# Six down-projection matmuls ahead of a slab's last two products, and another token order for the first two row blocks

## The chip, the core and the metric

The kernel runs on one core of a Trainium2 chip. A core has a matrix engine (TensorE, called PE in the profile, with its weight loads as PEld), a vector engine (DVE), a scalar engine (ACT), a GpSimd engine (POOL) and a sync engine (SP) that here issues all large DMAs. The engines run side by side and wait for each other through semaphores. SBUF is the on-chip memory; PSUM holds the sums of the matmuls in eight banks. The metric is the device time of one execution in microseconds (us); lower is better.

## What is computed

Two layers, each a gated feed-forward block, a mixer (convolution, linear recurrence, windowed attention) and a second gated feed-forward block, each followed by a residual layer norm, on 512 tokens of width 1024 in float32. The change touches the feed-forward blocks alone, of which there are four:

```python
def _swiglu(x, wg, wu, wd):
    return (jax.nn.silu(x @ wg) * (x @ wu)) @ wd
...
    for l in range(DEPTH):
        h = 0.5 * _swiglu(x, ffn_w_gate[l, 0], ffn_w_up[l, 0], ffn_w_down[l, 0])
        x = _layernorm(ALPHA * x + h, ln_g[l, 0], ln_b[l, 0])
...
        h = 0.5 * _swiglu(x, ffn_w_gate[l, 1], ffn_w_up[l, 1], ffn_w_down[l, 1])
        x = _layernorm(ALPHA * x + h, ln_g[l, 2], ln_b[l, 2])
```

`x` is 512 x 1024, `wg` and `wu` are 1024 x 2816, `wd` is 2816 x 1024.

## The kernel before

**Numbers in two parts.** A float32 product is made from three matmuls: each operand is split into a rounded part (`wh`, `hH`: the high part) and the rest (`wl`, `hL`). `split` (L128) does this with an ACT cast (L130) and then a DVE subtraction (L131), so a weight tile costs one load by DMA, one ACT cast and one DVE subtraction before PE can use both parts.

**Slabs.** A feed-forward block works through its 2816 hidden columns in three slabs (`SLABS`, L43) of 4, 4 and 3 pairs of 256 columns (the very first pair of a block is done apart). Four blocks of three slabs make twelve slab ends; in eight of them another slab of the same block follows, and four are the last of their block (`fin`, L486).

**First half of a slab: products.** Each pair's gate and up projections are made by a scheme that needs seven products of half-size blocks in place of eight. The products have names: p1, p2, q6, p5, p7, p4, q3. Each is 24 matmuls (L481 to L483) with 256 moving columns. They share PSUM banks: p1, q6, p7 and p4 of one pair add up one after the other in one bank, p5 and q3 in another, and p2 has a third (L503). Between two products of a bank its sum so far is taken out: by an ACT copy after p1 (L510), q6 (L515), p7 (L517) and p4 (L520), and by DVE after p7 (L518, from the bank of p5) and q3 (L523). `seq` (L550 to L554) is the order of the products. Inside a slab the p4 and q3 of one pair come after the p1 of the next pair. For the last pair of a slab there is no next pair, and the order ends p5, p7, p4, q3, so that p4 follows p7 directly in the same bank.

**Weights of the products** are made ready (`prep`, L427) `AHEAD` = 3 products early (L557 to L560): when p5 of the last pair runs, q3's weights are prepared, and nothing is left to prepare in `seq`. The raw gate and up weights of a pair lie in buffers of `tpool` (L408, DMAs of L411, two per buffer); as soon as one of them comes free, the next slab's raw weights are fetched into it.

**Second half of a slab: the down projection.** For each row block f of `wd` (128 of its rows, 4 KB each; a slab has 8, 8 or 6) the block is loaded and split (`load_rows`, L386, its DMA is L365), and for each t of the four blocks of 128 tokens `rowmm` (L453) adds six matmuls with 512 moving columns into the two PSUM banks `ys[t]`: two of `hL` with `wh`, then four of `hH` with `wl` and `wh`. In the trace these are L107. The eight banks of `ys` are all the banks there are. The first row block of a slab is f0, its hidden columns are those of the slab's first pair, finished long before the slab's end. In the last slab the last four row blocks go by tokens instead of by f, into the layer norm.

**Order and buffers.** The program is written as one sequence; when it is built, a list scheduler puts the instructions of each engine in an order by priority (place in the program) and by when it believes that they can start. Each engine then runs its own list strictly from the front, and SP its DMAs. Buffers of a pool (`wpool` has 15 of 4 KB per partition: raw, high and low weights, the products' outputs `o` and sums) are handed out in the program's order of first use: a tile gets its buffer only after every tile that is first written earlier in the program has got one. The raw, `wh` and `wl` of a row block are three such tiles; `ob`, the tile which the ACT copy after p7 (L517) writes first, is another.

Of the kernel before, what the change touches and what calls it, by code (L numbers as in the profile page):

```python
# [18 lines left out]
P = 128  # L19
D = 1024  # L20
S = 512
NT = S // P
# [30 lines left out]
def tile_hymba(  # L53
# [39 lines left out]
    def nm(s):  # L93
        uid[0] += 1
        return f"{s}_{uid[0]}"

    def bank():
        return psum.tile([P, 512], F32, tag="ps", name=nm("ps"))
# [7 lines left out]
    def mm(o, a, b, start, stop):  # L106
        nc.tensor.matmul(o, a, b, start=start, stop=stop)  # L107
# [25 lines left out]
    def transposed(dst, q, j, src):  # L133

        pt = bank()
        for c in range(4):
            nc.tensor.transpose(pt[:, c * P:(c + 1) * P], src[:, c * P:(c + 1) * P], ident)  # L137
        sl = slice(j * P, j * P + P)
        split(dst[q][:, 0, :, sl], dst[q][:, 1, :, sl], pt.rearrange("p (c t) -> p c t", c=4))
# [179 lines left out]
    class Start:  # L319
# [6 lines left out]
        def load(self, n=1, pool=None):  # L326
            for _ in range(n):
                self.pairs.append(self.thunks.pop(0)(pool))
# [57 lines left out]
    def load_rows(src, c, pool=None):  # L386
        return load(src[c * P:(c + 1) * P, :], pool)
# [65 lines left out]
    def rowmm(ys, a, w, first, last):  # L453
        ah, al = a
        wh, wl = w
        for hf in range(2):
            sl = slice(hf * 512, (hf + 1) * 512)
            mm(ys[hf], al, wh[:, sl], first, False)
        for hf in range(2):
            sl = slice(hf * 512, (hf + 1) * 512)  # L460
            mm(ys[hf], ah, wl[:, sl], False, False)
            mm(ys[hf], ah, wh[:, sl], False, last)

    def ffn(l, i, idx, start, nxt, last, hooks={}):
        wd = w_down[l, i]
# [8 lines left out]
        def product(step, n, pb, first):  # L474
            src, q = A[step]
            wh, wl = pairs[n].ready.pop(step)
            for g in range(2):
                o = pb[:, g * HALF:(g + 1) * HALF]
                for k in range(4):
                    st = first and g == 0 and k == 0  # L480
                    nc.tensor.matmul(o, wl[:, g, k, :], src[q][:, 0, k, :], start=st, stop=False, skip_group_check=True)  # L481
                    nc.tensor.matmul(o, wh[:, g, k, :], src[q][:, 1, k, :], start=False, stop=False, skip_group_check=True)  # L482
                    nc.tensor.matmul(o, wh[:, g, k, :], src[q][:, 0, k, :], start=False, stop=k == 3, skip_group_check=True)  # L483

        for si, (n0, n1) in enumerate(SLABS):
            fin = si == len(SLABS) - 1  # L486
            f0, f1 = 2 * n0, 2 * n1
            hH = hpool.tile([P, HMAX, S], F32R, tag="hA", name=nm("hH"))
            hL = hpool.tile([P, HMAX, S], F32R, tag="hB", name=nm("hL"))

            def finish(n, which, tile_, s0):

                v = tile_.rearrange("p (b g s) -> p b g s", b=2, g=2)
                nc.scalar.activation(v[:, :, 0, :], v[:, :, 0, :], AF.Silu)
                nc.vector.tensor_tensor(v[:, :, 0, :], v[:, :, 0, :], v[:, :, 1, :], op=ALU.mult)
                f = 2 * (n - n0)
                sl = (slice(None), slice(f, f + 2), slice(s0, s0 + HALF))
                split(hH[sl], hL[sl], v[:, :, 0, :])

            def run(step, n):  # L500
                if step in ("p1", "p2", "p5"):
                    acc[step, n] = bank()
                pb = acc[{"p1": "p1", "q6": "p1", "p7": "p1", "p4": "p1", "p2": "p2", "p5": "p5", "q3": "p5"}[step], n]  # L503
                product(step, n, pb, step in ("p1", "p2", "p5"))
                if step == "p1":
                    outs[n] = [wpool.tile([P, D], F32, tag="w", name=nm("o")) for _ in range(2)]
                oa, ob = outs[n]
                lo, hi = slice(0, 512), slice(512, 1024)
                if step == "p1":
                    nc.scalar.copy(oa[:, lo], pb)  # L510
                elif step == "p2":
                    nc.vector.tensor_tensor(oa[:, lo], pb, oa[:, lo], op=ALU.add)
                    acc.pop(("p2", n))
                elif step == "q6":
                    nc.scalar.copy(oa[:, hi], pb)  # L515
                elif step == "p7":
                    nc.scalar.copy(ob[:, hi], pb)  # L517
                    nc.vector.tensor_tensor(ob[:, hi], acc["p5", n], ob[:, hi], op=ALU.subtract)  # L518
                elif step == "p4":
                    nc.scalar.copy(ob[:, lo], pb)  # L520
                    finish(n, 1, ob, HALF)
                elif step == "q3":
                    nc.vector.tensor_tensor(oa[:, hi], pb, oa[:, hi], op=ALU.subtract)  # L523
                    finish(n, 0, oa, 0)
                    acc.pop(("p5", n))
                    acc.pop(("p1", n))
                    outs.pop(n)

            m4 = []
            first = n0 + 1 if si == 0 else n0  # L530
            if si == 0:
# [18 lines left out]
            seq = []  # L550
# [4 lines left out]
            ready = 0  # L555
            for m, (step, n) in enumerate(seq):
                while ready < min(len(seq), m + 1 + AHEAD):  # L557
                    st, k = seq[ready]
                    pairs[k].prep(st)
                    ready += 1  # L560
                    if st == "p5" and k + 1 < n1:
                        pairs[k + 1].raw(0, 0)
                        pairs[k + 1].raw(1, 0)
                run(step, n)
                if m4:
                    transposed(sT, 2, 2 - len(m4), m4.pop(0))
                if step == "q3" and n in hooks:
                    hooks[n]()
            if fin:
                extra.pop()  # L570
            ys = [[bank(), bank()] for _ in range(NT)]

            def hpair(f, t):
                return hH[:, f - f0, t * P:(t + 1) * P], hL[:, f - f0, t * P:(t + 1) * P]

            flow = f1 - RESIDENT if fin else f1
            for f in range(f0, flow):
                w = load_rows(wd, f)
                for t in range(NT):
                    rowmm(ys[t], hpair(f, t), w, f == f0, f == f1 - 1)  # L580
            if not fin:
                for t in range(NT):
                    for hf, sl in enumerate(HS):
# [9 lines left out]
            def rows(t):  # L593
                for w, f in zip(ws, range(flow, f1)):
                    rowmm(ys[t], hpair(f, t), w, f == f0, f == f1 - 1)
                return ys[t]
# [332 lines left out]
    for l in range(DEPTH):  # L929
        phases += [(ffn, (l, 0, 3 * l), ffn_start(l, 0)), (mixer, (l, 3 * l + 1), mixer_start(l)),  # L930
                   (ffn, (l, 1, 3 * l + 2), ffn_start(l, 1))]
# [61 lines left out]
```

## Time and profile before

| | us |
|---|---|
| median of 3 runs | 1787.61 (1785.95 to 1791.46) |
| the profiled execution | 1785.95 |
| its span, first to last instruction | 1784.2 |
| mean granted TensorE clock | 0.994 of full speed |

A row of the profile names line, engine, operation, and out<-in tiles; L107 is the helper `mm`, so those rows are told apart by their tiles (`hH`, `hL` only occur in the down projection). A matmul row's duration overlaps the next one's: a stream's pace is the distance between two starts. A timeline row is: start, duration, engine, line, operation, tiles, shape, count, and in square brackets how long the engine had been idle and what ended that. A row with x4 merges four instructions. SP's rows are DMA issues; the transfer itself lasts longer.

### The profile page before, as it was taken

How to read it: one execution, taken by the hardware profiler on the slowest of the kernel's cores; microseconds unless marked ns; L12 is line 12 of the kernel's file. 1: busy time of each engine (PE TensorE's matmuls, PEld its weight loads, DVE VectorE, ACT ScalarE, POOL GpSimd, SP SyncE). 2: the span in 40 equal slices, each digit the busy share in tenths (PEclk: the TensorE clock that was granted, in tenths of full speed). 3: DMA queues.
4: the chain of work that ended last, by engine and by line, in shares of the span. 5: the costliest groups of instructions: out<-in, count | busy, mean ns of one | idle time of the engine just before them, and what ended most of it. 6: DMA issues, size and time to landing. Idle time of an engine off the chain costs nothing. (4 is left out here: it accounts for less than half of the span.)

```text
span 1784.2 us, 27912 instructions
## 1 busy us (share of the span) xinstructions
PE 1730.9 (97%) x11538; PEld 1564.1 (88%) x11538; DVE 1279.1 (72%) x1777; ACT 824.2 (46%) x1224; POOL 41.8 (2%) x76
## 2 busy tenths in 40 slices
PE   8999999999999999999999999999999999999997
PEld 8988989988579989989889899898876899899896
DVE  5856756769977856857588567575898877587475
ACT  4543443533854643534445345254458445255252
POOL 0200000010000000000000000000000000000000
PEclk9999999999999999999999999999999999999999
DMA  5341542322322442422334324223321244135122
GB/s 157 108 142 57 159 135 69 108 79 66 98 82 63 130 141 60 128 97 72 107 92 122 130 71 136 78 72 108 106 66 60 71 130 149 57 104 165 44 87 72
DMA packets 236840, 177.34 MB, mean 99 GB/s; under 512 B 9524, under 2 KB 219561, under 8 KB 236713
## 3 DMA queue, kind: packets, MB, share of 16 engines
q1 hardware_dynamic: 236712, 175.55, 32.3%
q8 instruction: 91, 1.49, 0.3%
q14 instruction: 37, 0.30, 0.1%
HBM read 171.33 MB, written 3.67 MB: 98 GB/s over the span
## 5 line engine op out<-in xcount | busy, mean ns | idle before, releaser
L131 DVE TENSOR_TENSOR wl<-raw,wh 128x1024 fp32r<-128x1024 f32 x268 | 324.8, 1221 | 151.8 <-ACT wh L130 118.0
L481 PE MATMUL ps<-xT,wl 128*128 128x256 f32 x1280 | 359.1, 281 | 9.4 <-ACT o L517 8.8
L482 PE MATMUL ps<-xT,wh 128*128 128x256 f32 x1280 | 356.9, 279 | 0.0
L483 PE MATMUL ps<-xT,wh 128*128 128x256 f32 x1280 | 356.7, 279 | 0.0
L130 ACT CAST wh<-raw 128x1024 fp32r<-128x1024 f32 x268 | 278.5, 1049 | 122.3 <-DMA raw<-in_ffn_w_down_dram 58.6
L131 DVE TENSOR_TENSOR wl<-t,wh 128x1024 fp32r<-128x1024 f32 x160 | 195.8, 1226 | 144.1 <-ACT wh L130 118.4
L107 PE MATMUL ps<-wl,hH 128*128 128x512 f32 x704 | 274.7, 390 | 1.1 <-DVE wl L131 1.1
L107 PE MATMUL ps<-wh,hH 128*128 128x512 f32 x704 | 274.3, 390 | 0.0
L481 PE MATMUL ps<-sT,wl 128*128 128x256 f32 x960 | 269.1, 280 | 4.9 <-ACT o L510 4.9
L482 PE MATMUL ps<-sT,wh 128*128 128x256 f32 x960 | 268.7, 280 | 0.0
L483 PE MATMUL ps<-sT,wh 128*128 128x256 f32 x960 | 268.5, 280 | 0.0
L481 PEld LDWEIGHTS ps<-xT,wl 128*128 128x128 f32 x1280 | 241.8, 189 | 13.8 <-ACT o L517 11.1
L130 ACT CAST wh<-t 128x1024 fp32r<-128x1024 f32 x160 | 167.1, 1052 | 178.7 <-DVE t L419 143.6
L482 PEld LDWEIGHTS ps<-xT,wh 128*128 128x128 f32 x1280 | 241.8, 189 | 0.3
L483 PEld LDWEIGHTS ps<-xT,wh 128*128 128x128 f32 x1280 | 241.8, 189 | 0.0
L107 PE MATMUL ps<-xT,wh 128*128 128x256 f32 (+1 forms) x960 | 216.9, 321 | 2.2 <-DVE xT L131 2.2
L107 PE MATMUL ps<-wh,hL 128*128 128x512 f32 x704 | 217.2, 390 | 0.5 <-ACT wh L130 0.4
L481 PEld LDWEIGHTS ps<-sT,wl 128*128 128x128 f32 x960 | 180.6, 188 | 6.9 <-ACT o L510 5.8
L483 PEld LDWEIGHTS ps<-sT,wh 128*128 128x128 f32 x960 | 180.6, 188 | 0.0
L482 PEld LDWEIGHTS ps<-sT,wh 128*128 128x128 f32 x960 | 180.4, 188 | 0.0
L107 PEld LDWEIGHTS ps<-xT,wh 128*128 128x128 f32 x960 | 160.1, 191 | 17.9 <-DVE xT L131 3.2
L107 PEld LDWEIGHTS ps<-wl,hH 128*128 128x128 f32 x704 | 132.2, 188 | 29.9 <-DVE wl L131 2.5
(165 smaller groups left out, 2333.1 us busy)
## 6 DMA issues: line engine op xcount, KB each, us to landing
raw<-in_ffn_w_down_dram SPq DMA_DIRECT2D x88, 512.0 KB
raw<-in_ffn_w_gate_dram SPq DMA_DIRECT2D x160, 256.0 KB
raw<-in_ffn_w_up_dram SPq DMA_DIRECT2D x160, 256.0 KB
raw<-in_w_in_dram SPq DMA_DIRECT2D x28, 512.0 KB
raw<-in_w_out_dram SPq DMA_DIRECT2D x16, 512.0 KB
raw<-in_ffn_w_gate_dram SPq DMA_DIRECT2D x8, 512.0 KB
raw<-in_ffn_w_up_dram SPq DMA_DIRECT2D x8, 512.0 KB
t<-in_ln_g_dram SPq DMA_DIRECT2D x6, 512.0 KB
```

The costliest lines, as they stand in the source:

```text
L107: nc.tensor.matmul(o, a, b, start=start, stop=stop)
L130: nc.scalar.copy(hi, src)
L131: nc.vector.tensor_tensor(lo, src, hi.bitcast(F32), op=ALU.subtract)
L481: nc.tensor.matmul(o, wl[:, g, k, :], src[q][:, 0, k, :], start=st, stop=False, skip_group_check=True)
L482: nc.tensor.matmul(o, wh[:, g, k, :], src[q][:, 1, k, :], start=False, stop=False, skip_group_check=True)
L483: nc.tensor.matmul(o, wh[:, g, k, :], src[q][:, 0, k, :], start=False, stop=k == 3, skip_group_check=True)
```

## The change

Four things are changed in `ffn`:

1. `load_rows(wd, f0)`, the load and split of the slab's first row block, stands in the program right after q3's weights have been prepared, ahead of the products p5, p7, p4 and q3 of the last pair. Before, it stood behind them all.
2. The six matmuls of row block f0 for the first 128 tokens, `down(f0, 0)`, are written ahead of `run` of the last product but one, which is p4: the order is p7, `down(f0, 0)`, p4, q3. So they stand between p7 and p4, in front of the last two products.
3. The other seven groups of six of the first two row blocks go in the order (f0, t 1), (f0, 2), (f0+1, 0), (f0+1, 1), (f0+1, 2), (f0, 3), (f0+1, 3); before, all of f0 came first and then all of f0+1.
4. The banks `ys[t]` are taken when they are first needed instead of all eight at once. Row blocks from f0+2 on go as before.

No instruction is added or taken away.

```diff
+            ys = {}
+            early = {}
+
+            def hpair(f, t):
+                return hH[:, f - f0, t * P:(t + 1) * P], hL[:, f - f0, t * P:(t + 1) * P]
+
+            def down(f, t):
+                if t not in ys:
+                    ys[t] = [bank(), bank()]
+                rowmm(ys[t], hpair(f, t), early[f], f == f0, f == f1 - 1)
...
+                if ready == len(seq) and f0 not in early:
+                    early[f0] = load_rows(wd, f0)
+                if m == len(seq) - 2:
+                    down(f0, 0)
                 run(step, n)
...
-            ys = [[bank(), bank()] for _ in range(NT)]
...
-            for f in range(f0, flow):
-                w = load_rows(wd, f)
+            early[f0 + 1] = load_rows(wd, f0 + 1)
+            for f, t in ((f0, 1), (f0, 2), (f0 + 1, 0), (f0 + 1, 1), (f0 + 1, 2), (f0, 3), (f0 + 1, 3)):
+                down(f, t)
+            for f in range(f0 + 2, flow):
+                early[f] = load_rows(wd, f)
                 for t in range(NT):
-                    rowmm(ys[t], hpair(f, t), w, f == f0, f == f1 - 1)
+                    down(f, t)
```

More of the change, by code (lines that the diff above doesn't have):

```diff
@@ L570, in ffn @@
                 extra.pop()
-            ys = [[bank(), bank()] for _ in range(NT)]
-            def hpair(f, t):
-                return hH[:, f - f0, t * P:(t + 1) * P], hL[:, f - f0, t * P:(t + 1) * P]
             flow = f1 - RESIDENT if fin else f1
-            for f in range(f0, flow):
-                w = load_rows(wd, f)
+            early[f0 + 1] = load_rows(wd, f0 + 1)
[3 more added lines that the diff above has]
+                early[f] = load_rows(wd, f)
                 for t in range(NT):
-                    rowmm(ys[t], hpair(f, t), w, f == f0, f == f1 - 1)
+                    down(f, t)
             if not fin:
```

## The prediction

> **What bounds the kernel now.** I read the page first, then the list of waits, then the timeline around the slab ends, engine by engine.
>
> ```profile
> PE 1730.9 (97%) x11538; PEld 1564.1 (88%) x11538; DVE 1279.1 (72%) x1777; ACT 824.2 (46%) x1224; POOL 41.8 (2%) x76
> PEclk9999999999999999999999999999999999999999
> ```
> ```profile
> PEld ps L481 <- ACT o L517: 11.1, 12, 0.9
> ...
> PE ps L481 <- ACT o L517: 8.8, 12, 0.7
> ```
>
> PE is busy 97% of the span, at full clock in every slice. What can be won is therefore a PE wait, and the list of waits names one that occurs exactly twelve times: a product's first matmul (L481) waits for the copy of L517. Twelve is the number of slab ends. PE's timeline at one of the eight slab ends that another slab follows shows what it costs:
>
> ```profile
> 1506.56 0.28 PE L482 MATMUL ps<-sT,wh 128*128 128x256 f32 x1
> 1506.67 0.28 PE L483 MATMUL ps<-sT,wh 128*128 128x256 f32 x1
> 1507.68 0.38 PE L481 MATMUL ps<-xT,wl 128*128 128x256 f32 x1 [0.73 <-ACT o L517]
> ```
>
> Product matmuls start 0.11 to 0.12 us apart, so p7's stream ends at 1506.67 + 0.12 = 1506.79, and p4 begins at 1507.68: **0.89 us** lost. p4 adds into the bank that the copy has still to read. Twelve such stalls are 10.7 us. Six down matmuls between p7 and p4 would fill such a gap, if their weights are there. So the question is when row block f0 is ready, and the answer lies in the other engines' rows at the same place (ACT, DVE, SP):
>
> ```profile
> 1503.47 1.05 ACT L130 CAST wh<-t 128x1024 fp32r<-128x1024 f32 x1 [1.48 <-DVE t L419]
> 1504.42 1.04 ACT L130 CAST wh<-raw 128x1024 fp32r<-128x1024 f32 x1
> 1507.04 0.58 ACT L517 COPY o<-ps 128x512 f32<-128x512 f32 x1 [1.57 <-PE ps L483]
> ...
> 1511.36 1.05 ACT L130 CAST wh<-raw 128x1024 fp32r<-128x1024 f32 x1
> ```
> ```profile
> 1505.69 1.22 DVE L131 TENSOR_TENSOR wl<-raw,wh 128x1024 fp32r<-128x1024 f32 x1
> 1507.66 0.69 DVE L518 TENSOR_TENSOR o<-ps,o 128x512 f32<-128x512 f32 x1 [0.75 <-ACT o L517]
> 1512.44 1.23 DVE L131 TENSOR_TENSOR wl<-raw,wh 128x1024 fp32r<-128x1024 f32 x1 [4.09 <-ACT wh L130]
> ```
> ```profile
> 1503.44 0.37 SPq L411 DMA_DIRECT2D raw<-in_ffn_w_gate_dram  x1
> 1503.86 0.51 SPq L411 DMA_DIRECT2D raw<-in_ffn_w_up_dram  x1
> 1506.94 0.37 SPq L411 DMA_DIRECT2D raw<-in_ffn_w_gate_dram  x1
> 1507.41 0.44 SPq L365 DMA_DIRECT2D raw<-in_ffn_w_down_dram  x1
> ```
>
> Read from below: f0's DMA is issued at 1507.41, its cast runs at 1511.36, its subtraction at 1512.44 to 1513.67. The casts at 1503.47 and 1504.42 are p4's and q3's weights; q3's subtraction ends at 1506.91. At 1506.79, when the changed program wants f0, its DMA has not even been issued.
>
> **The change part by part.** No instruction is added; what counts is where each stands in its queue.
>
> *How early f0's load can come.* Buffers of wpool go out in program order of first use. In the new program the raw tile of f0 follows directly on q3's `wl`, so its DMA can be placed once q3's subtraction has been given its buffer, when that begins (1505.69 here). The gate and up pair at 1503.44 and 1503.86 had its buffer before that and stays ahead in SP's queue; the gate DMA of 1506.94 waits for the buffer that q3's subtraction frees at its end, so f0 goes in front of it. SP is done with the pair at 1503.86 + 0.51 = 1504.37, and f0's issue falls there, at 1504.4 (p5 has just given two buffers back). The DMA passed over is 0.4 us later; it fetches for the next slab, which begins behind this one's eight row blocks.
>
> *How long it takes.* Issue to cast:
>
> ```profile
> 98.01 0.46 SPq L365 DMA_DIRECT2D raw<-in_ffn_w_down_dram  x1
> ```
> ```profile
> 103.43 1.05 ACT L130 CAST wh<-raw 128x1024 fp32r<-128x1024 f32 x1 [1.52 <-DMA raw<-in_ffn_w_down_dram]
> ```
> ```profile
> 1517.76 1.69 SPq L365 DMA_DIRECT2D raw<-in_ffn_w_down_dram  x2
> ```
> ```profile
> 1521.32 1.05 ACT L130 CAST wh<-raw 128x1024 fp32r<-128x1024 f32 x1 [1.48 <-DMA raw<-in_ffn_w_down_dram]
> ```
>
> The bounds are 5.42 us (98.01 to 103.43, four transfers crowding it) and 3.56 us (1517.76 to 1521.32). I take 3.95 (1507.41 to 1511.36), since there as here a gate and up pair is in flight beside it: f0 is cast from 1508.35.
>
> *From the cast to PE*, taken from the one place where PE already waits for f0, the first slab end:
>
> ```profile
> 103.84 0.28 PE L483 MATMUL ps<-sT,wh 128*128 128x256 f32 x1
> 104.53 0.73 PE L107 MATMUL ps<-wh,hL 128*128 128x512 f32 x2 [0.41 <-ACT wh L130]
> 105.79 0.50 PE L107 MATMUL ps<-wl,hH 128*128 128x512 f32 x1 [0.53 <-DVE wl L131]
> 106.13 0.39 PE L107 MATMUL ps<-wh,hH 128*128 128x512 f32 x1
> 106.36 0.39 PE L107 MATMUL ps<-wl,hH 128*128 128x512 f32 x1
> ```
> ```profile
> 104.51 1.23 DVE L131 TENSOR_TENSOR wl<-raw,wh 128x1024 fp32r<-128x1024 f32 x1 [5.64 <-ACT wh L130]
> ```
>
> The first `hL` matmul starts 1.10 us after the cast does, the first `wl` matmul 1.28 after the subtraction does, which itself starts 1.08 after the cast: 2.36 in all. A down matmul takes 0.23.
>
> *The eight slab ends with a slab behind them.* PE wants f0 at 1506.79 and gets it at 1508.35 + 1.10 = 1509.45: a stall of **2.66**. Two `hL` matmuls, to 1509.91. `wl` is there at 1508.35 + 2.36 = 1510.71. The copy of L517 is in the meantime late too: its tile is first used behind f0's three in program order, so it stands behind f0's cast on ACT. It starts 0.95 after the cast (as the casts of 1503.47 and 1504.42 do), at 1509.30, and p4 may start 0.64 later (1507.04 to 1507.68), at 1509.94. Between 1509.94 and 1510.71 only p4 has matmuls ready. If the build puts some of p4 there, 0.2 is lost for gaps; if it keeps the six together, all of 1510.71 − 1509.91 = 0.80. I take 0.2, because PE's order already mixes two streams where one isn't ready:
>
> ```profile
> 176.79 0.84 PE L107 MATMUL ps<-t,t 33*128 33x384 f32 x1
> 177.56 0.58 PE L481 MATMUL ps<-sT,wl 128*128 128x256 f32 x1
> 178.07 1.65 PE L107 MATMUL ps<-t,t 33*128 33x384 f32 x2
> ```
>
> So 2.86 in place of 0.89: **+1.97 each, +15.8 for eight** (+20.6 with the six kept together). Queued behind the waiting cast are L517 on ACT and behind the subtraction L518 on DVE; for them wait p4 (counted) and q3, whose bank L518 reads, and p4's 2.8 us cover that.
>
> *The four last slabs of a block* fetch no further pairs, and SP is not held up (the rows are SP, ACT, DVE, PE):
>
> ```profile
> 1727.36 12.56 SPq L365 DMA_DIRECT2D raw<-in_ffn_w_down_dram  x5
> ```
> ```profile
> 1730.64 1.05 ACT L130 CAST wh<-raw 128x1024 fp32r<-128x1024 f32 x1
> 1733.24 0.58 ACT L517 COPY o<-ps 128x512 f32<-128x512 f32 x1 [1.55 <-PE ps L483]
> ```
> ```profile
> 1731.91 1.22 DVE L131 TENSOR_TENSOR wl<-raw,wh 128x1024 fp32r<-128x1024 f32 x1
> ```
> ```profile
> 1732.87 0.28 PE L483 MATMUL ps<-sT,wh 128*128 128x256 f32 x1
> 1733.88 0.38 PE L481 MATMUL ps<-xT,wl 128*128 128x256 f32 x1 [0.73 <-ACT o L517]
> ```
>
> f0 is issued at 1727.36 already and lands by 1731.3. Its cast follows q3's, at 1731.59, and is done before p7 ends (1732.99): the two `hL` matmuls run without a wait, to 1733.45, and p4 goes on at 1733.88 as now. `wl` follows q3's subtraction, at 1731.91 + 1.14, and serves PE from 1734.33, inside p4. A stall of 0.43 for 0.89: **−0.46 each, −1.8 for four** (0 with the six kept together).
>
> *What goes at the first two slab ends.* At the first PE now loses 0.57 ahead of 104.53 (0.69 less a pace of 0.12) and 0.80 ahead of 105.79 (1.26 less two matmuls). The second has 0.24 and 0.80:
>
> ```profile
> 238.86 0.28 PE L483 MATMUL ps<-sT,wh 128*128 128x256 f32 x1
> 239.22 0.73 PE L107 MATMUL ps<-wh,hL 128*128 128x512 f32 x2
> 240.48 0.50 PE L107 MATMUL ps<-wl,hH 128*128 128x512 f32 x1 [0.53 <-DVE wl L131]
> ```
>
> By then f0 has been there for two products: **−2.4**.
>
> *The other token order* I cost at nothing. f0+1 is wanted two groups (2.7 us) after q3 rather than four, but q3 itself ends 1.97 + 1.37 later, and f0+1's load moves up behind f0's: more slack than before. t 3 comes last, so q3's and p4's banks have 6.9 us to be emptied instead of 4.1. If that cover failed, it would be a wait of about 1 us at each end.
>
> *Sum:* 15.8 − 1.8 − 2.4 = **+11.6 us**. On the profiled execution's 1785.95 that is 1797.6; the median of the runs is 1.7 above it, so on the median 1787.6 + 11.6 = **1799.2**.
>
> [...]
>
> **The rivals.**
>
> *The weights come in time* (faster). If the load is placed early enough at all twelve ends, each is like the last slabs: 12 × −0.46 − 2.4 = −7.9, 1779.7; with the whole gap filled −10.7 − 2.4 = −13.1, 1774.5. It decides at an issue before about 1502, so that the cast comes directly behind q3's. For it speaks that the DMA queue has room then; against it the buffers' order, and that DVE has work to 1506.91 anyhow. Chance 0.17.
>
> *Nothing moves.* The build might place p4 ahead of the six matmuls, as these are not ready: then 0.89 stays, and −2.4 or nothing changes: 1785.2 to 1787.6. Against it: L517's tile comes behind f0's, so p4 isn't ready either. 0.12.
>
> *The load stays behind the gate DMA of 1506.94*: issue 1507.41, PE at 1511.36 + 1.10 = 1512.46, a stall of 5.67 + 0.2, +4.98 each, 39.8 − 4.2 = +35.6, 1823. 0.08.
>
> *The clock falls.* A stall this long may cost PE its full clock. Were each p4 behind it at half pace (24 × 0.12 more), the eight ends would cost 23 us more: 1822. In the page every slice has full clock, but no stall of this length stands among products. 0.04.
> [...]
>
> **How the numbers follow.** The forecast has 0.59. Its own range: loads of 3.56 give 8 × 0.39 = 3.1 less (1796), 5.42 gives 8 × 1.47 = 11.8 more (1811), the six kept together 6.6 more (1806): 1793 to 1812. The range down to the faster rival's 1779 and up to 1813 leaves out the two slow rivals and a little of the fast one: 1779 to 1813. A measurement tells about 0.3%, 5.4 us, from no change. Faster by more: 0.17. Within: 0.12 and 0.02 of the forecast. Slower by more: 0.69.
>
> **What would show it.** In the changed profile the wait of L481 for L517 has gone or become short, and in its place the first `hL` matmul of f0 (L107, `ps<-wh,hL`) waits for ACT's `wh`, eight times for over 2 us and four times hardly. ACT has f0's cast ahead of L517. SP issues f0 about 2.4 us before p7 ends, ahead of a gate DMA. Wrong would be: an issue of f0 before p5; a PE order with all of p4 ahead of the down matmuls; a new wait at f0+1 or at the banks of t 3.

## The result and the profile after

| | before | after |
|---|---|---|
| median of the runs, us | 1786.78 (4 runs, 1783.42 to 1791.46) | 1810.62 (4 runs, 1807.36 to 1814.12) |
| the profiled execution, us | 1785.95 | 1814.12 |
| its span, us | 1784.2 | 1812.3 |
| mean granted TensorE clock | 0.994 | 0.981 |

The ratio is **1.0141** (95% interval 1.0123 to 1.0159): 24 us slower, where 11.6 were forecast. The direction held; the loss was twice the size. From the page of the changed kernel, PE's busy time and the granted clock in 40 slices:

```profile
PE 1748.6 (96%) x11538; PEld 1578.0 (87%) x11538; DVE 1280.3 (71%) x1777; ACT 825.9 (46%) x1224; POOL 40.8 (2%) x76
PEclk9999999999899999999999999999999999999999
```

The same 11538 matmuls keep PE busy 17.7 us longer than before (1748.6 for 1730.9): part of the loss is no wait, but slower matmuls. The list of PE's waits, of the changed kernel (us in total, times, longest):

```profile
PE ps L107 <- ACT wh L130: 31.1, 9, 4.6
...
PE ps L137 <- DVE xs L305: 2.7, 6, 0.7
```

and the same two rows of the kernel before:

```profile
PE ps L137 <- DVE xs L305: 8.4, 6, 1.7
...
PE ps L107 <- ACT wh L130: 0.4, 1, 0.4
```

The wait of L481 for L517, 8.8 us in twelve, has no row any more. In its place the down projection's first matmuls wait for the cast of `wh`, 31.1 us in nine. And a wait that the prediction did not speak of has become shorter: L137, the transposes of a new block's input, behind the layer norm (L305).

**One slab end of the changed kernel**, the same one that the prediction shows of the kernel before (there p7's last matmul starts at 1506.67, here at 1526.93). Its timeline on PE:

```profile
1526.93 0.28 PE L483 MATMUL ps<-sT,wh 128*128 128x256 f32 x1
1530.49 1.65 PE L107 MATMUL ps<-wh,hL 128*128 128x512 f32 x3 [3.28 <-ACT wh L130]
1531.94 0.41 PE L481 MATMUL ps<-xT,wl 128*128 128x256 f32 x1
1532.15 0.41 PE L482 MATMUL ps<-xT,wh 128*128 128x256 f32 x1
...
1533.00 0.63 PE L107 MATMUL ps<-wl,hH 128*128 128x512 f32 x1
1533.43 0.63 PE L107 MATMUL ps<-wh,hH 128*128 128x512 f32 x1
...
1536.77 0.28 PE L481 MATMUL ps<-xT,wl 128*128 128x256 f32 x1
1536.89 0.28 PE L482 MATMUL ps<-xT,wh 128*128 128x256 f32 x1
```

PE stands from 1526.93 + 0.12 = 1527.05 to 1530.49, **3.44 us** (2.66 were forecast). Then the next 6 us run at half pace: product matmuls start 0.21 apart (1531.94, 1532.15) and not 0.12 (1536.77, 1536.89), down matmuls 0.43 (1533.00, 1533.43) and not 0.23. (The row with x3 holds f0's two `hL` matmuls for the first 128 tokens and one of the next group.) On ACT and on SP at the same place:

```profile
1524.68 1.04 ACT L130 CAST wh<-raw 128x1024 fp32r<-128x1024 f32 x1
1529.39 1.04 ACT L130 CAST wh<-raw 128x1024 fp32r<-128x1024 f32 x1 [3.67 <-DMA raw<-in_ffn_w_down_dram]
1530.34 0.58 ACT L517 COPY o<-ps 128x512 f32<-128x512 f32 x1
```
```profile
1523.72 0.37 SPq L411 DMA_DIRECT2D raw<-in_ffn_w_gate_dram  x1
1524.14 0.50 SPq L411 DMA_DIRECT2D raw<-in_ffn_w_up_dram  x1
1524.75 0.44 SPq L365 DMA_DIRECT2D raw<-in_ffn_w_down_dram  x1
1527.19 0.37 SPq L411 DMA_DIRECT2D raw<-in_ffn_w_gate_dram  x1
```

The queues stand as forecast: f0's DMA goes behind the first pair and ahead of the gate DMA that was at 1506.94 before; f0's cast stands ahead of L517. Only the landing takes 1529.39 − 1524.75 = 4.64 us instead of 3.95.

**The clock.** Busy time by stretches of 3.41 us at that place (the stretch, its length, busy us and instructions of PE, PEld, DVE, ACT and POOL, then the granted clock, the DMA share and GB/s; PE's idle time in a stretch is the length less PE's busy time):

```profile
1523.01:1526.42 3.41, 3.41 (x32) 3.41 (x31) 2.24 (x3) 2.00 (x2) 0.00 (x0) 1.00 0.43 127
1526.42:1529.83 3.41, 0.79 (x7) 0.59 (x6) 0.74 (x1) 0.44 (x1) 0.00 (x0) 1.00 0.81 244
1529.83:1533.24 3.41, 2.75 (x9) 2.46 (x10) 1.82 (x2) 1.09 (x2) 0.00 (x0) 0.50 0.93 297
1533.24:1536.65 3.41, 3.41 (x14) 3.02 (x14) 0.76 (x1) 1.04 (x1) 0.00 (x0) 0.50 0.64 253
1536.65:1540.07 3.42, 3.42 (x31) 3.42 (x30) 1.16 (x2) 1.26 (x3) 0.00 (x0) 1.00 0.46 153
```

The granted clock is exactly a half in two whole stretches and full before and behind. Half clock follows all eight stalls: a clock of 0.50 begins at 99.64, 239.59, 642.36, 772.07, 1004.18, 1130.47, 1529.83 and 1659.54. In the kernel before it begins at 174.51, 1259.94 and 1775.36 (behind the last matmul), at no slab end.

**The books.** For every PE matmul I took the distance from its start to the next start, less the pace of its size (0.228, 0.117 and 0.109 us for 512, 256 and 128 columns), and added these excesses up by place. "Slab ends" reach from 100 matmuls ahead of a down projection to 60 behind its start; "block ends" from there to the next block's products; "tail" is the time from the last matmul's start to the span's end.

| us | before | after | difference |
|---|---|---|---|
| slab ends | 14.5 | 50.9 | +36.4 |
| block ends | 16.9 | 6.0 | −10.9 |
| tail | 12.1 | 10.4 | −1.7 |
| elsewhere | 48.0 | 52.3 | +4.3 |
| span | 1784.2 | 1812.3 | +28.1 |

The eight first stalls of slab ends, each read as the one above, are 3.75, 3.79, 4.74, 3.90, 3.61, 3.70, 3.44 and 4.25 us: 31.2, a mean of **3.90**. Half clock behind them costs 14.3 (for each matmul in such a stretch but the first behind the stall, its distance less the pace; with that first one 16.5). What remains of 50.9 is 5.4. "Elsewhere" holds half clock that differs from run to run, as the mean clocks of the kernel before do (0.988 to 0.996 in its runs beside the experiments; its profile has 10.2 us of it from 174.5 on, inside the first block, the changed one as much at 178 and again at 485, in a mixer); I count it as no part of the change. The profiled execution is the slowest of the four after, so the medians differ by 23.8 and not by 28.1.

### The profile page after: what moved, and what is told of

It reads as the page before. It is cut to its first block, busy times and chain, and to the rows that moved or that the text cites. A ratio compares the mean times of both kernels' runs of the same rounds, so it can differ in the third digit from the quotient of the medians.

```text
span 1812.3 us, 27913 instructions
## 1 busy us (share of the span) xinstructions
PE 1748.6 (96%) x11538; PEld 1578.0 (87%) x11538; DVE 1280.3 (71%) x1777; ACT 825.9 (46%) x1224; POOL 40.8 (2%) x76
## 3 DMA queue, kind: packets, MB, share of 16 engines
q8 instruction: 91, 1.49, 0.3%
## 4 chain that ended last, share of the span: by engine, by line
PE 64%; DVE 20%; ACT 6%; DMA 5%; issue 3%; POOL 1%; SPq 0%; DVEq 0%; POOLq 0%; ACTq 0%
PE ps L107 43%; PE ps L481 6%; PE ps L482 6%; PE ps L483 6%; DVE t L419 6%; DVE wl L131 5%; ACT wh L130 4%; DMA raw<-in_ffn_w_down_dram 2%; DMA raw<-in_ffn_w_up_dram 2%; DVE hL L131 2%; DVE o L495 1%; PE ps L137 1%; DVE t L289 1%; DVE xs L305 1%; DVE o L523 1%
## 5 line engine op out<-in xcount | busy, mean ns | idle before, releaser
L481 PE MATMUL ps<-xT,wl 128*128 128x256 f32 x1280 | 361.7, 283 | 0.7 <-DVE wl L131 0.5
L107 PE MATMUL ps<-wl,hH 128*128 128x512 f32 x704 | 276.9, 394 | 0.1
L107 PE MATMUL ps<-wh,hH 128*128 128x512 f32 x704 | 276.3, 393 | 0.0
L481 PE MATMUL ps<-sT,wl 128*128 128x256 f32 x960 | 269.2, 280 | 4.9 <-ACT o L510 4.9
L107 PE MATMUL ps<-wh,hL 128*128 128x512 f32 x704 | 224.2, 401 | 31.1 <-ACT wh L130 31.1
L481 PEld LDWEIGHTS ps<-xT,wl 128*128 128x128 f32 x1280 | 245.5, 192 | 5.6 <-ACT o L517 1.4
L107 PE MATMUL ps<-xT,wh 128*128 128x256 f32 (+1 forms) x960 | 215.6, 320 | 0.9 <-DVE xT L131 0.9
L481 PEld LDWEIGHTS ps<-sT,wl 128*128 128x128 f32 x960 | 180.7, 188 | 6.9 <-ACT o L510 5.8
L107 PEld LDWEIGHTS ps<-wh,hL 128*128 128x128 f32 x704 | 133.7, 192 | 59.1 <-ACT wh L130 32.9
L107 PEld LDWEIGHTS ps<-xT,wh 128*128 128x128 f32 x960 | 159.0, 190 | 16.1 <-DVE xT L131 1.3
```

## The experiments

Each is a change of the changed kernel unless it says "of the kernel before". The ratios are to the kernel before on the same chip: 1786.95 beside the first four, 1784.94 beside the next three, 1783.92 beside the last three.

### Which part of the change is it: the token order or the load?

*Order only.* The new token order stays; f0's load and all groups go back behind q3:

```diff
-                if ready == len(seq) and f0 not in early:
-                    early[f0] = load_rows(wd, f0)
-                if m == len(seq) - 2:
-                    down(f0, 0)
                 run(step, n)
...
+            early[f0] = load_rows(wd, f0)
             early[f0 + 1] = load_rows(wd, f0 + 1)
-            for f, t in ((f0, 1), (f0, 2), ...
+            for f, t in ((f0, 0), (f0, 1), (f0, 2), ...
```

> Only the other token order of the first two row blocks is kept; f0's load and its first six matmuls stand behind q3 as before. Theory (the late load of f0 makes the loss): within 0.3% of before, 1782 to 1792 us, clock 0.99. Rival (the token order makes new waits, at f0+1's weights or at the banks of t 3): a good part of the 25 us, 1797 to 1812.

*Load only.* The early load stays; all down groups stand behind q3 in the old order:

```diff
                 if ready == len(seq) and f0 not in early:
                     early[f0] = load_rows(wd, f0)
-                if m == len(seq) - 2:
-                    down(f0, 0)
...
-            early[f0 + 1] = load_rows(wd, f0 + 1)
-            for f, t in ((f0, 1), (f0, 2), ...
-                down(f, t)
-            for f in range(f0 + 2, flow):
+            for t in range(NT):
+                down(f0, t)
+            for f in range(f0 + 1, flow):
```

> Only the early load of f0 is kept; all down matmuls stand behind q3 in the old token order. Theory (the copy of L517 gets its buffer behind f0's three tiles and so stands behind f0's cast on ACT): p4 still waits about 4 us at eight slab ends, now for the copy, the clock still falls behind it, and the time is like the changed kernel's, 1803 to 1818. Rival (the six matmuls between p7 and p4 are what waits, the load alone is harmless): 1780 to 1792, p4's wait 0.9 us as before.

Measured: order only 1785.89, ratio 0.9997 [0.9981, 1.0013]. Load only 1808.46, ratio 1.0118 [1.0086, 1.0150]. PE's waits with the order only:

```profile
PE ps L481 <- ACT o L517: 8.8, 12, 0.8
PE ps L137 <- DVE xs L305: 8.4, 6, 1.7
```

and with the load only:

```profile
PE ps L107 <- ACT wh L130: 30.0, 9, 4.2
...
PE ps L137 <- DVE xs L305: 3.4, 6, 0.7
```

The token order costs nothing, as forecast. The early load alone makes the loss, without a single line of the program that puts the six matmuls ahead of p4: with L517 behind f0's cast neither p4 nor f0 is ready, and the build itself then puts f0's first matmuls there. It also brings the shorter wait at L137, which the order alone does not.

### Is it the order in which buffers are handed out?

L517 is behind f0's cast, said the prediction, because its tile `ob` is first used behind f0's three tiles. One small write to `ob` on GpSimd ahead of the load turns this around (L517 overwrites it) and leaves the rest:

```diff
                 if ready == len(seq) and f0 not in early:
+                    nc.gpsimd.memset(outs[n][1][:, 0:1], 0.0)
                     early[f0] = load_rows(wd, f0)
```

> The changed kernel with one small write to the tile of L517 in front of f0's load, so that this tile has its buffer first and the copy may stand ahead of f0's cast. Nothing else is moved. Theory: the build now has p4 ready before f0 and puts most of it ahead of the six matmuls; p4's wait of 0.9 us is back at twelve ends, the 4 us waits and the half clock are gone, 1780 to 1792. Rival (the load's late landing holds PE whatever the order of buffers): still over 1800.

Measured: 1785.86, ratio 0.9992 [0.9976, 1.0008]: the whole loss is gone. The timeline of ACT at the same slab end:

```profile
1502.03 1.05 ACT L130 CAST wh<-raw 128x1024 fp32r<-128x1024 f32 x1
1504.64 0.58 ACT L517 COPY o<-ps 128x512 f32<-128x512 f32 x1 [1.56 <-PE ps L483]
1507.14 1.05 ACT L130 CAST wh<-raw 128x1024 fp32r<-128x1024 f32 x1 [1.92 <-DMA raw<-in_ffn_w_down_dram]
```

L517 now runs as soon as p7 ends, and f0's cast behind it. p4 waits 0.73 as in the kernel before and then covers most of f0's landing. So most of the new stall is not the price of an f0 that comes late, but of all PE's work standing behind it. What the late f0 still costs here, and the wait at L137, which is not as short as in the changed kernel, stand in PE's waits:

```profile
PE ps L107 <- ACT wh L130: 5.8, 8, 1.4
PE ps L137 <- DVE xs L305: 5.7, 6, 1.7
```

### Is the half clock a cost of its own?

The eight stalls are filled with matmuls: 16 of product size go into a spare bank between p7 and the six of f0. Their result is not used, and they make the work longer by 8 × 16 × 0.117 = 15 us, where PE only waited.

```diff
+            if step == "p7":
+                kept.append((wh, wl))
...
                 if m == len(seq) - 2:
+                    if not fin:
+                        spare = bank()
+                        for j in range(16):
+                            nc.tensor.matmul(spare[:, :HALF], kept[-1][0][:, 0, j % 4, :], sT[1][:, 0, j % 4, :],
+                                             start=j == 0, stop=j == 15)
                     down(f0, 0)
```

> The changed kernel with 16 more product matmuls (about 1.9 us of work whose result is not used) between p7 and the six, at the eight slab ends with a slab behind them. Theory (a stall near 4 us also costs half clock behind it, 14 us in all): PE's idle time there falls to about 2 us, the clock stays full, and the time falls by 10 to 15 us against the changed kernel, 1795 to 1801, although PE has more to do. Rival (the clock has no part, only the wait counts): the added matmuls lie in the wait and the time stays at 1807 to 1814.

Measured: 1798.80 (1797.79 to 1801.50), ratio 1.0070 [1.0046, 1.0095]: with more matmuls, 11.8 us faster than the changed kernel. At two of the eight ends (first two pairs of rows) the clock still fell, at the other six it did not (two are shown). Columns as above:

```profile
232.67:236.08 3.41, 1.34 (x12) 1.15 (x11) 0.00 (x0) 0.03 (x1) 0.00 (x0) 1.00 0.72 229
236.08:239.50 3.42, 2.35 (x8) 2.08 (x9) 1.83 (x2) 2.10 (x3) 0.00 (x0) 0.50 0.99 327
761.74:765.15 3.41, 1.44 (x9) 1.11 (x8) 1.17 (x2) 1.53 (x2) 0.00 (x0) 1.00 0.83 271
765.15:768.56 3.41, 3.41 (x14) 3.02 (x13) 0.66 (x2) 0.80 (x1) 0.00 (x0) 0.50 0.88 331
99.55:102.96 3.41, 1.94 (x11) 1.72 (x12) 1.83 (x2) 1.53 (x2) 0.00 (x0) 1.00 0.98 284
...
635.44:638.85 3.41, 1.71 (x11) 1.38 (x11) 0.83 (x1) 1.53 (x2) 0.00 (x0) 1.00 0.80 254
```

In the books the slab ends cost 23.1 + 15 = 38.1 us instead of 50.9. The eight stalls that are left sum to 16.1 us (1.89, 3.29, 1.85, 2.13, 1.58, 1.93, 1.62, 1.80); with the 15 of filling that is the 31.2 of waiting before, so these 12.8 us are nearly all clock: with the first matmul behind each stall counted in, half clock at the slab ends costs 16.5 us in the changed kernel and 4.3 here, at the two ends that fell, 12.2 less.

### The four last slabs and the eight others, each alone

The change is made only where a slab is its block's last, and then only where it is not:

```diff
-                if ready == len(seq) and f0 not in early:
-                    early[f0] = load_rows(wd, f0)
-                if m == len(seq) - 2:
-                    down(f0, 0)
+                if fin:
+                    if ready == len(seq) and f0 not in early:
+                        early[f0] = load_rows(wd, f0)
+                    if m == len(seq) - 2:
+                        down(f0, 0)
...
-            early[f0 + 1] = load_rows(wd, f0 + 1)
-            for f, t in ((f0, 1), (f0, 2), ...
-                down(f, t)
-            for f in range(f0 + 2, flow):
+            if fin:
+                early[f0 + 1] = load_rows(wd, f0 + 1)
+                for f, t in ((f0, 1), (f0, 2), ...
+                    down(f, t)
+            for f in range(f0 + 2 if fin else f0, flow):
```

> The change made only in the last slab of each block (four ends), the eight others as before. Theory (there the early load comes in time, and with the later row blocks' loads also moved up, the build lets the tokens finish one after the other, so that the layer norm starts sooner): excess over PE's pace at the block ends falls from 17 to about 6 us and the tail behind the last matmul by 1 to 2 us; 1770 to 1778. Rival (the gain at the block ends in the changed kernel came from elsewhere, as from the delay of all that lies ahead of it): 1782 to 1788.

In the other kernel `not fin` stands for `fin`:

> The change made only at the eight slab ends with a slab behind them, the last slabs as before. Theory (the losses all lie there, and the gains of the last slabs are missing): the changed kernel's time plus about 12 us, 1818 to 1828, with half clock behind most of the eight stalls. Rival (the two places are not independent): 1805 to 1814, like the changed kernel.

Measured: last slabs alone 1772.26, ratio 0.9945 [0.9925, 0.9964]; the others alone 1822.26, ratio 1.0217 [1.0196, 1.0239]. Together −11.7 + 38.3 = +26.6, about the whole change's 24. PE's waits with the last slabs alone:

```profile
PE ps L481 <- ACT o L517: 5.8, 8, 0.7
...
PE ps L137 <- DVE xs L305: 2.8, 6, 0.7
```

and with the others alone:

```profile
PE ps L107 <- ACT wh L130: 28.7, 8, 4.1
PE ps L137 <- DVE xs L305: 8.4, 6, 1.7
...
PE ps L481 <- ACT o L517: 2.9, 4, 0.7
```

The slab ends bring 14.5 − 12.8 = 1.7 us in the books, near the forecast's 1.8, but that is partly luck: end by end, only about 1 us of it lies at the last slabs (three fall from 0.97 to 0.35, one rises from 0.98 to 1.92), and the rest at the eight other ends, which this kernel leaves as they were (the first of them took 1.2 in place of 2.5). The same kernel wins 10.9 at the block ends and 2.5 in the tail, which the forecast had not at all. The eight other ends cost 48.2 − 14.5 = 33.7.

### If f0 is there in time, or p4 is covered otherwise

*Fetched early.* f0's raw tile comes from the other pool (`tpool`) and is fetched seven products before the slab's end; its split stays where the change has it:

```diff
+                if m == len(seq) - 7:
+                    raw0 = tpool.tile([P, D], F32, tag="t", name=nm("raw"))
+                    nc.sync.dma_start(raw0, wd[f0 * P:(f0 + 1) * P, :])
                 if ready == len(seq) and f0 not in early:
-                    early[f0] = load_rows(wd, f0)
+                    early[f0] = load(None, None, raw0)
```

> The changed kernel with f0's raw weights fetched into a buffer of tpool right behind the preparation of p5, two products earlier; its cast and subtraction stay behind q3's preparation. Theory (only the late landing is at fault): f0 lands before p7 ends at all twelve ends, PE waits 0.4 to 0.9 us there for f0's subtraction, no half clock at slab ends; 1777 to 1785, 0.2 to 0.5% faster than before. Rival (the fetch into tpool delays the next slab's weights, or other waits remain): 1787 or more.

*Split early too.* With that fetch, the split goes ahead of q3's preparation:

```diff
+                    if ready == len(seq) - 1:
+                        early[f0] = load(None, None, raw0)
...
-                if ready == len(seq) and f0 not in early:
-                    early[f0] = load_rows(wd, f0)
+                if m == len(seq) - 7:
+                    raw0 = tpool.tile([P, D], F32, tag="t", name=nm("raw"))
+                    nc.sync.dma_start(raw0, wd[f0 * P:(f0 + 1) * P, :])
```

> As the kernel with the early fetch, and f0's cast and subtraction also stand ahead of q3's preparation. Theory: the six matmuls run without a wait directly behind p7 and hide the copy of L517 in full; 12 x 0.89 + 2.4 = 13 us less than before, 1771 to 1776. Rival (q3's weights are now late by the time of one split, 1.2 us): the gain is smaller or gone, 1780 or more, with a wait of q3 for its weights.

*Another cover, of the kernel before.* No down matmul moves; p2 of a slab's last pair, a product with a bank of its own, goes between p7 and p4:

```diff
-            seq += [("p4", n1 - 1), ("q3", n1 - 1)]
+            seq.remove(("p2", n1 - 1))
+            seq += [("p2", n1 - 1), ("p4", n1 - 1), ("q3", n1 - 1)]
```

> The kernel before with one thing moved: the last pair of a slab has its p2 between p7 and p4, in place of six down matmuls; p2 has a bank and weights of its own. Theory (any matmuls that are ready hide the copy of L517): the wait of L481 for L517 is gone at twelve ends, 10.7 us less, 1774 to 1779; f0's waits at the first two ends stay. Rival (q6 now follows q3 of the pair before more closely and something else becomes late): 1783 or more.

*Both.* p2 between p7 and p4, f0 fetched and split early, all down groups behind q3 in the order of the kernel before (the lines are set against the changed kernel):

```diff
-            seq += [("p4", n1 - 1), ("q3", n1 - 1)]
+            seq.remove(("p2", n1 - 1))
+            seq += [("p2", n1 - 1), ("p4", n1 - 1), ("q3", n1 - 1)]
...
+                    if ready == len(seq) - 1:
+                        early[f0] = load(None, None, raw0)
...
-                if ready == len(seq) and f0 not in early:
-                    early[f0] = load_rows(wd, f0)
-                if m == len(seq) - 2:
-                    down(f0, 0)
+                if m == len(seq) - 7:
+                    raw0 = tpool.tile([P, D], F32, tag="t", name=nm("raw"))
+                    nc.sync.dma_start(raw0, wd[f0 * P:(f0 + 1) * P, :])
...
-            early[f0 + 1] = load_rows(wd, f0 + 1)
-            for f, t in ((f0, 1), (f0, 2), ...
-                down(f, t)
-            for f in range(f0 + 2, flow):
+            for t in range(NT):
+                down(f0, t)
+            for f in range(f0 + 1, flow):
```

> p2 of the last pair between p7 and p4, and f0 fetched and split early as in the kernel with the split ahead of q3's preparation, but with all its matmuls behind q3 in the old token order. Theory (p2 hides the copy, the early load brings the tokens of the last slab into order): the slab ends of the one and the block ends of the other, 2 to 5 us less than either, 1756 to 1760. Rival (both hide the same thing): 1761 to 1764.

| | median, us | ratio | slab ends | block ends | tail |
|---|---|---|---|---|---|
| before | | | 14.5 | 16.9 | 12.1 |
| fetched early | 1766.19 | 0.9897 [0.9881, 0.9914] | 8.9 | 6.7 | 9.8 |
| split early too | 1761.13 | 0.9869 [0.9853, 0.9885] | 1.0 | 6.8 | 9.8 |
| p2 between | 1763.70 | 0.9886 [0.9869, 0.9904] | −1.2 | 10.3 | 11.0 |
| p2 and early f0 | **1754.67** | **0.9835 [0.9817, 0.9854]** | −1.0 | 3.9 | 8.4 |

(The pace is a rounded mean, so a sum may fall a little below nothing.) All four beat their expectations: at the slab ends they bring about what was expected (p2 between more), and the block ends bring the rest. The fetch alone missed one point: at the first block's last slab PE still stood 1.3 us for f0, with half clock behind it (0.50 from 334.74 on). With fetch and split early the change does what it says. With p2 as the cover it isn't needed at all: 24 matmuls that are ready and have a bank of their own hide L517 (PE's list has no row of that wait, 8.8 us before). The last kernel's rows, from the page:

```profile
PE 1720.4 (98%) x11538; PEld 1558.4 (89%) x11538; DVE 1278.5 (73%) x1777; ACT 822.3 (47%) x1224; POOL 43.9 (3%) x76
```

and from PE's waits:

```profile
PE ps L137 <- DVE xs L305: 0.5, 1, 0.5
```

It is 1.65% faster than the kernel before and has neither a wait for L517 nor one for f0's `wh`.

## Why the prediction was right in sign and wrong in size

**Right: what moves, and where to.** f0's issue (2.3 us ahead of p7's end, 2.4 forecast), its place between the two pairs on SP, the cast ahead of L517 on ACT, and PE's order (p7, `hL`, five of p4, the four other down matmuls, the rest of p4, q3) came as worked out. Moving `ob` in the buffers' order shows that this order is the cause. The last slabs' ends were worth about 1 of the 1.8: three of the four have no stall ahead of the `hL` matmuls and win 0.6 each, where 0.46 was forecast, and one has a stall of 1.31 and loses 0.9. The waits of the first two ends have gone: the list has no row of L107 waiting for DVE's `wl`. The token order is nothing.

**Wrong, first: the landing, 3.95 us.** From issue to cast the eight took 4.89, 5.01, 5.93, 5.13, 4.82, 4.93, 4.64 and 5.14, a mean of 5.06. This is the term "How long it takes"; 1.11 more than 3.95; with some 0.13 from a later issue the stalls are 3.90 and not 2.66, 8 × 1.24 = **9.9 us** too little. The two bounds, 3.56 and 5.42, hold seven of the eight. (The ends of the stated own range, 1793 and 1812, lie some 3 and 1 us outside its terms, 1796 and 1811, with no reason given.) The chosen row had one half of a pair ahead of f0 (gate at 1506.94) and the other behind (up at 1507.90); in its new place f0 follows a whole pair, issued 1.03 and 0.61 us before it. That this is why it lands later was not tried by itself.

**Wrong, second: the rival "the clock falls" was true, and had 0.04.** All eight stalls were followed by half clock, which cost **14.3 us**. The rival's price, 23, took all of p4 at half pace; it lasted one stretch of 3.41 us at four ends and two at the others. The failed step is that the clock stands in the sum with nothing, because every slice of the page has full clock and because no stall of this length stood among products. The first reason misreads the page: a 9 there is 90% or more, and the kernel before has half clock too, from 174.5 on and at a block end:

```profile
1256.53:1259.94 3.41, 1.71 (x15) 1.33 (x14) 2.98 (x5) 0.33 (x2) 1.31 (x2) 1.00 0.51 146
1259.94:1263.35 3.41, 3.41 (x19) 3.41 (x17) 3.16 (x9) 2.87 (x5) 0.37 (x2) 0.50 0.03 7
```

The idle 1.70 us of the first row are nearly all one wait of 1.67 (L137 for the layer norm): a gap shorter than 2.66, with half clock behind it. The second reason looked only at products, and this wait stands at a block end. The length of a gap alone did not decide it in these profiles: half clock came behind that 1.67 and, with the gaps filled, behind 2.13 and 3.29, but not behind 1.93. The eight drops of the changed kernel lie whole multiples of 3.4133 us apart (41, 159, 197, 265, 302, 419 and 457 of them from 99.64 on; 1529.83 − 99.64 is 419), and half clock lasted 3.41 or 6.83 us there. In the 3.41 us ahead of a drop PE's idle time was 2.07 to 3.39 us at the eight ends. With the gaps filled, the two ends with 2.07 and 1.97 fell, and the six with 1.70 or less in any of their stretches of 3.41 us did not. What a gap of 2.66 us costs ahead of p4 was not shown: none of the eight stalls was that short.

**Left out: the block ends, −10.9, and the tail, −1.7.** The prediction took the last slabs for four stalls and did not look behind them. The gain comes with the last slabs' part of the change: it is there with the last slabs alone and with the load alone, not with the order alone and not with the eight others alone. The early load as such is not enough and not needed for it: with `ob` first, f0's load stands as early, and L137 still waits 5.7 us, 1.7 at the longest; with p2 between nothing is loaded early, and that wait falls too:

```profile
PE ps L137 <- DVE xs L305: 4.6, 3, 1.5
```

What goes with it is the order that the build then chooses: in the changed kernel the last row blocks run nearly token by token. Before, the tokens' last groups were mixed, two tokens ended at almost the same time, and their layer norms queued up on the way to L137. The last block's layer norms and matmuls show it, first on ACT before:

```profile
1763.78 1.15 ACT L294 ACTIVATE junk<-t,nmean 128x1024 bf16<-128x1024 f32 x1 [15.80 <-DVE nmean L292]
...
1777.46 1.15 ACT L294 ACTIVATE junk<-t,nmean 128x1024 bf16<-128x1024 f32 x1 [3.32 <-DVE nmean L292]
```

on PE before:

```profile
1772.10 0.39 PE L107 MATMUL ps<-wh,hH 128*128 128x512 f32 x1
```

and on ACT and PE after:

```profile
1789.54 1.15 ACT L294 ACTIVATE junk<-t,nmean 128x1024 bf16<-128x1024 f32 x1 [11.93 <-DVE nmean L292]
...
1805.06 1.15 ACT L294 ACTIVATE junk<-t,nmean 128x1024 bf16<-128x1024 f32 x1 [3.93 <-DVE nmean L292]
```
```profile
1801.91 0.39 PE L107 MATMUL ps<-wh,hH 128*128 128x512 f32 x1
```

Counted from the last matmul's start, the first token's layer norm runs 12.4 us ahead instead of 8.3, and the last one 3.2 us behind it instead of 5.4. Some 1.5 of the 10.9 is the half clock at 1259.94 shown above. Why the build chose the mixed order, that its estimate had the last row blocks' weights come too late, is argued from the program and was not tried.

**The sum.** Forecast +11.6, landing +9.9, clock +14.3, small waits at the slab ends +0.6, block ends −10.9, tail −1.7, elsewhere +4.3: +28.1, the difference of the spans. That the median came no higher than 1810.6 is owed to a gain that was not forecast, against two losses of twice that size.

## What to carry to other kernels

Work that is moved ahead to fill a gap brings its load, its split and its buffers with it; ask first what its buffers come ahead of, because here the copy that everything waited for was pushed behind a DMA. If a gap of 0.9 us is to be filled, take work that is already on chip (another product with its own bank) before work that has still to be fetched. The length of a gap was not its whole price here: the eight stalls, 31.2 us in all, cost 14.3 more in the half clock behind them. And what a slab's end does to the order at the far end of its block belongs in the sum (−10.9 here).

## What the hardware showed that was not expected

At the eight slab ends full clock came back after 3.41 us when PE had stood for 0.45 us or less of them (four ends) and after 6.83 when it had stood for 0.66 or more of the first 3.41 (the other four). The edge of a drop is not sharp in these numbers: 1.70 us of idle time stood ahead of one in the kernel before, as shown, and 1.70 ahead of none with the gaps filled (635.44 to 638.85, and 1.00 in the 3.41 us behind); in the kernel with f0 fetched early one drop came behind 1.49 (331.33 to 334.74). Idle time is not the whole of it either. The kernel before drops to half clock at 174.51 and the changed kernel at 178.15, each inside the first block and for 10.24 us, behind 3.41 us that PE's rows fill (171.10 to 174.51 and 174.74 to 178.15; in the kernel before mostly matmuls on 33 rows that build the attention's bias); what brings it there was not tried. A 512 KB load that took 3.56 us from issue to cast in one place of the kernel before (1517.76 to 1521.32) took up to 5.93 at a slab end of the changed one.
